# Raw z through DRAM with its silu at the gating, and q, k and v stored by pairs of heads

## The chip, the cores and the metric

The kernel runs on one core of a Trainium2 chip. The metric is device time in microseconds (us), the median of several runs: 641.59 us before the change (three runs, 641.56 to 641.76). Lower is better. Two such medians can be told apart when they differ by about 0.2%, some 1.3 us.

## What is computed

One layer of a diffusion transformer, in fp32, for 1024 latent tokens (a grid of 16 rows by 64 columns), 256 context tokens and a model width of 1024. Cut to what matters:

```python
h  = rmsnorm(x, norm_g) * (1 + scale) + shift          # 1024 tokens
hc = rmsnorm(ctx, norm_g) * (1 + scale_c) + shift_c    # 256 context tokens
q, k, v, za, u, bg, cg, zc = split(h @ w_in)           # eight parts of 512 columns
kc, vc = split(hc @ w_in[:, 512:1536])
q, k, kc = rmsnorm per head                            # 8 heads of 64
# each token sees a window of 8 x 16 neighbours (rotary q and k, learned bias)
# and all 256 context keys (plain q), in one softmax
attn = neighbourhood_attention(q, k, v, kc, vc, rpb) * silu(za)
conv = bg * conv3(cg * u) * silu(zc)
out  = x + gate * (concat([attn, conv]) @ w_out)
```

The change concerns the gate silu(za) of the attention half, and the way by which q, k and v get from the projection to the attention.

## The kernel before, in words

**Precision.** Every fp32 operand of a product is split into a high and a low part (`halves`, line 188: a copy on ScalarE to the rounded high part, a subtraction on VectorE for the low one). A product is three matmuls (`mm3`, line 72). Within a head's scores the two parts lie on the two halves of the 128 partitions: head dimension 64, times two.

**Stages.** First the modulation and the norms. Then the projection (loop at line 1170): for each of four pairs of heads, eight tiles of 128 tokens give 384 columns of q, k and v (`proj_tile`, line 283). Then the attention (line 1287) and at last the output projection (from line 1356 on). Through the projection q, k, v are normed, rotated, transposed, split, and written to DRAM with `spill`, which only notes a transfer; `flush` (line 1166) issues them on SyncE's queue (SP) one tile later. In the attention they come back head by head with `load_k`, `load_q` and `load_v` (lines 944 to 967). q and k of one head fill 64 rows in DRAM; they are loaded twice, to the upper and the lower 64 partitions. v carries a 65th column (ones in the high part, zeros in the low part) that gives the sums of the softmax; it is set once on chip (line 1263), so the transfers of v leave it out and move pieces of 64 floats.

**The quarters.** The attention is a software pipeline over 36 steps, called quarters, four to a head (`quarter`, line 1066). Quarter n computes the scores of group n (`pss` for the window, `pc` for the context), the maxima and exponentials of group n-2, and the products with v of group n-3 (`po`). The order of all instructions on TensorE, ScalarE, VectorE and GpSimd is as written by hand here (`strict`, line 1289); the order of SP's transfers is the scheduler's. Within a quarter ScalarE copies the row maxima (`mg`), which VectorE then subtracts from the scores, and computes the exponentials (`phc`, `sc`, `phl`, `sb`).

**Fillers.** Between these steps TensorE works through the other columns of w_in, in units of 128 columns (`unit`, line 338); one unit has eight ticks, a tick is six matmuls into the bank `pu`. `TICKS` (line 33) says how many ticks each quarter takes: 3 as a rule, 2 in quarters 0, 5 and 8, 4 in quarters 17, 18, 27, 28 and 32, 33. The first four units are the z columns of the four pairs (`attn_group`, line 484), the others belong to three convolution groups (`conv_group`, line 384). Work on the other engines that follows a unit is queued as chores and done at fixed places of a quarter: `do_acts` at its end, `do_dves` near its start.

**The gate.** `attn_group` takes the silu of z from the two banks of a finished unit and stores it (`zs_d`). Once both heads of a pair are done, `gated` (line 1267) advances by one step in each quarter: it loads the sums, takes the reciprocal, stores it, loads silu(z), the attention's output and the reciprocals, multiplies, and stores the product in `y_d`. The last pair is gated in the output stage instead (`put_y`, line 1334).

## Time and profile before

| quantity | value |
|---|---|
| median of three runs | 641.59 us |
| profiled execution, its own time | 643.59 us |
| span in the profile of that execution | 641.8 us |
| TensorE, VectorE, ScalarE, GpSimd busy | 98%, 67%, 50%, 20% of the span |
| DMA, queue of SP | 112,348 packets, 113.23 MB |
| packets under 512 B, all queues | 32,817 of 118,864 |
| attention | from about 270 us to about 535 us of the span |

Times within the span are in us from its start. The profiled execution takes 1.8 us more than its span, and 2.0 us more than the median. In the lists of instructions a row gives start, duration, engine, line, operation, written tile <- read tiles, shape and count; in square brackets stands how long the engine had been idle and on whom it waited. Most lines read L55, that of a helper, so tiles are what to go by. In a table of windows each row gives the stretch, its length, then the busy time of each engine with its count of instructions, the granted clock of TensorE, the busy share of the 16 DMA engines and the bytes moved per second. The matmuls are pipelined, so TensorE looks busy through short gaps; the length of a quarter tells more than its busy time.

### The profile page before, as it was taken

What the parts mean: (1) busy time and instruction counts of PE and PEld (TensorE: products, weight loads), DVE (VectorE), ACT (ScalarE), POOL (GpSimd) and SP (SyncE); (2) the same over time, 40 slices, a digit from 0 to 9 for tenths busy, and PEclk for the clock granted to TensorE, in tenths of its full rate; (3) what the DMA queues carried; (4) which work ended last, traced back from release to release, by engine and by line L of the source; (5) the groups of instructions that cost most, each with busy time, mean ns of one, the idle gap of its engine ahead of it and who ended that gap; (6) DMA issues with size and microseconds to landing.
All of it is one profiled execution on the core that took longest, in us unless ns stands there. A gap on an engine that the chain in (4) does not pass through costs nothing.

```text
span 641.8 us, 10295 instructions
## 1 busy us (share of the span) xinstructions
PE 629.1 (98%) x3480; PEld 537.3 (84%) x3480; DVE 432.3 (67%) x819; ACT 322.5 (50%) x692; POOL 131.5 (20%) x138
## 2 busy tenths in 40 slices
PE   8999999999999999999999999999999999999997
PEld 3477899999899999777688878888888888888885
DVE  1677859665756756458697889988998864565111
ACT  3676835424525444346676648565675644352000
POOL 1205024123123222001111211121111111004421
PEclk9999999999999999999999999999999999999999
DMA  8973647867785897899767758885862223965621
GB/s 319 379 257 97 180 121 259 256 188 206 241 260 165 271 269 218 216 221 223 184 160 195 186 140 212 202 214 149 225 150 88 71 81 128 293 235 198 215 100 49
DMA packets 118864, 125.46 MB, mean 195 GB/s; under 512 B 32817, under 2 KB 89353, under 8 KB 117532
## 3 DMA queue, kind: packets, MB, share of 16 engines
q1 hardware_dynamic: 112348, 113.23, 61.4%
q10 hardware_dynamic: 6208, 11.05, 5.5%
q0 software_dynamic: 256, 0.54, 0.3%
q8 instruction: 27, 0.44, 0.3%
q14 instruction: 25, 0.20, 0.1%
HBM read 88.01 MB, written 38.53 MB: 197 GB/s over the span
## 4 chain that ended last, share of the span: by engine, by line
PE 75%; DMA 10%; DVE 8%; SPq 3%; ACT 2%; issue 1%; ACTq 0%; DVEq 0%
PE pacc L55 21%; PE pu L55 18%; PE acc L55 5%; PE pout L76 5%; PE pout L74 5%; PE pout L75 5%; PE po L55 4%; PE tr L55 4%; PE cacc L55 4%; DMA v<-v_d 4%; DMA k_s<-k_d 3%; DVE mx L55 2%; DVE sb L55 2%; PE pss L55 2%; PE pmx L55 2%; DMA slab<-in_w_ada 2%
## 5 line engine op out<-in xcount | busy, mean ns | idle before, releaser
L55 PE MATMUL pu<-h,uh 128*128 128x512 f32 x544 | 169.0, 392 | 0.0
L55 PE MATMUL pacc<-wh,h 128*128 128x384 f32 x512 | 135.1, 338 | 0.0
L55 PEld LDWEIGHTS pu<-h,uh 128*128 128x128 f32 x544 | 98.2, 188 | 17.0
L55 PE MATMUL pu<-h,ul 128*128 128x512 f32 x272 | 106.3, 391 | 0.0
L55 PEld LDWEIGHTS pacc<-wh,h 128*128 128x128 f32 x512 | 92.8, 188 | 0.1
L55 POOL TENSOR_TENSOR plc<-sc,phc 128x512 fp32r<-128x512 f32 x32 | 42.5, 1327 | 222.8 <-ACT sc L55 111.4
L55 PE MATMUL pacc<-wl,h 128*128 128x384 f32 x256 | 85.6, 335 | 0.0
L55 POOL TENSOR_TENSOR ss<-ss,few 128x4 f32<-128x4 f32 (+1 forms) x40 | 42.0, 1051 | 125.8 <-DVE ss L55 125.4
L55 PEld LDWEIGHTS pu<-h,ul 128*128 128x128 f32 x272 | 51.1, 188 | 11.3
L55 DVE TENSOR_TENSOR mx<-mx,sb 128x384 f32<-128x384 f32 (+1 forms) x64 | 55.5, 876 | 1.9
L75 PE MATMUL pout<-wol,yh 128*128 128x512 f32 x128 | 49.8, 389 | 0.0
L76 PE MATMUL pout<-woh,yl 128*128 128x512 f32 x128 | 49.6, 389 | 0.0
L74 PE MATMUL pout<-woh,yh 128*128 128x512 f32 x128 | 48.3, 389 | 0.0
L55 PEld LDWEIGHTS pacc<-wl,h 128*128 128x128 f32 x256 | 48.1, 188 | 0.1
L55 DVE TENSOR_REDUCE ss<-sq 128x4 f32<-128x260 f32 (+1 forms) x40 | 15.7, 393 | 41.9 <-ACT sq L55 41.9
L55 ACT COPY mg<-pmx 128x256 f32<-128x256 f32 x32 | 12.0, 374 | 61.7 <-PE pmx L55 44.5
L55 ACT ACTIVATE sq<-pacc 128x256 f32<-128x256 f32 x32 | 12.3, 385 | 57.1 <-PE pacc L55 56.6
L1375 DVE TENSOR_TENSOR ot<-pout,gate 128x512 f32<-128x512 f32 x16 | 10.8, 688 | 37.6 <-PE pout L76 35.5
L55 DVE TENSOR_TENSOR pll<-sb,phl 128x768 fp32r<-128x768 f32 (+2 forms) x33 | 29.3, 889 | 7.9 <-ACT sb L55 7.9
L55 DVE TENSOR_TENSOR sc<-sc,mg 128x512 f32<-128x512 f32 x32 | 21.8, 683 | 19.0 <-ACT mg L55 19.0
L1376 POOL TENSOR_TENSOR ot<-ot,xr 128x512 f32<-128x512 f32 x15 | 20.0, 1347 | 67.6 <-DVE ot L1375 66.5
L55 ACT ACTIVATE qn<-pacc,ss 128x64 f32<-128x64 f32 x128 | 30.1, 329 | 4.7 <-issue 2.5
(151 smaller groups left out, 1277.0 us busy)
## 6 DMA issues: line engine op xcount, KB each, us to landing
uraw<-in_w_in SPq DMA_DIRECT2D x34, 256.0 KB
q_d<-qs SPq DMA_DIRECT2D x64, 128.0 KB
k_s<-k_d SPq DMA_DIRECT2D x16, 512.0 KB
q_s<-q_d SPq DMA_DIRECT2D x32, 256.0 KB
wr<-in_w_in SPq DMA_DIRECT2D x40, 192.0 KB
slab<-in_w_ada SPq DMA_DIRECT2D x6, 1024.0 KB
t_d<-btw SPq DMA_DIRECT2D x8, 576.0 KB
bt<-t_d SPq DMA_DIRECT2D x8, 576.0 KB
```

Source lines behind the costliest of these rows:

```text
L55: i = emit(*a, **kw)
L74: i = pe.matmul(ps, ah, bh, start=first, stop=False)
L75: pe.matmul(ps, ah, bl, start=False, stop=False)
L76: pe.matmul(ps, al, bh, start=False, stop=last)
L1375: dve.tensor_tensor(ot, ps, gate[:, cols], ALU.mult)
L1376: (dve if (nh, t) == (1, NB - 1) else pool).tensor_tensor(ot, ot, xr, ALU.add)
```

## The change

- z is copied raw from its bank, each half as soon as it is done, and stored (`z_d`). `gated` loads both halves in its first step; ScalarE takes their silu in place, through a list `held`, either with the next convolution group's silus (pair 0) or by a chore of its own (pairs 1 and 2). Pair 3 takes it in the output stage.
- `gated` makes both multiplications of a half in one step. The gated pairs form a queue; before, a new one took the place of the old one.
- q, k, v and the context's kc and vc are stored by pairs of heads, 128 rows to a transfer. k, q and kc are loaded with one transfer for both partition halves: the rows of high and low parts, or two copies of each row (`twice`), alternate over the partitions.
- v is stored with its 65th column, together with vc; a head's v comes in two transfers with runs of 650 floats in each partition.
- An Exp on a constant column is run on ScalarE three tiles before the end of the projection.
- In quarter 0 one tick of the filler goes ahead of the context's scores; its number of ticks stays 2.

```diff
-    q_d = many("q_d", NH, [2, HD, 4, 2, 256])
-    k_d = many("k_d", NH, [HD, 4, 2, 256])
-    v_d = many("v_d", NH, [P, 4, 2, 2 * HD])
-    kc_d = many("kc_d", NH, [HD, 2, L])
-    vc_d = many("vc_d", NH, [P, 2, 2 * HD])
+    q_d = many("q_d", NPAIR, [P, 2, 4, 2, 256])
+    k_d = many("k_d", NPAIR, [P, 4, 2, 256])
+    v_d = many("v_d", NPAIR, [P, 2, 2, NB + 2, HD + 1])
+    kc_d = many("kc_d", NPAIR, [P, 2, L])
...
+    def spill_v(p, b, vs):
+        spill(v_d[p][:, :, :, b:b + 2].rearrange("p s l b d -> p (s l) (b d)"), vs.rearrange("p s l i d -> p (s l) (i d)"))
...
-            for s in range(2):
-                h, rows = 2 * p + s, slice(64 * s, 64 * s + 64)
-                for l in range(2):
-                    spill(q_d[h][l, :, t0 // 2], qs[rows, l])
-                spill(k_d[h][:, t0 // 2], ks[rows])
+            for l in range(2):
+                spill(q_d[p][:, l, t0 // 2], qs[:, l])
+            spill(k_d[p][:, t0 // 2], ks)
...
     def silus(z):
         out = []
         for half, ps in z:
             out.append(cvp.tile([P, 512], F32, name="zs", tag="ub", bufs=2))
             act.activation(out[half], ps, AF.Silu)
+        while held:
+            for v in held.pop():
+                act.activation(v, v, AF.Silu)
         return out
...
     def attn_group(f):
-        z = []
+        def keep(half, ps):
+            z = cvp.tile([P, 512], F32, name="z", tag="ub", bufs=2)
+            act.copy(z, ps)
+            sp.dma_start(z_d[f][:, half * 512:(half + 1) * 512], z)
+
         for got in unit(z_col(f)):
             if got:
-                z.append(got)
+                chore(lambda got=got: keep(*got))
             else:
                 yield
-        def on_act():
-            for half, zs in enumerate(silus(z)):
-                sp.dma_start(zs_d[f][:, half * 512:(half + 1) * 512], zs)
-        chore(on_act)
...
+    def twice(rows):
+        n = 1
+        for step, size in list(rows.ap)[1:]:
+            n *= size
+        return bass.AP(rows.tensor, rows.offset, [[n, HD], [0, 2], [1, n]])
...
-            for i in range(2):
-                sp.dma_start(self.k[64 * i:64 * i + 64].bitcast(F32), k_d[h])
+            sp.dma_start(self.k[:].bitcast(F32).rearrange("p t l c -> p (t l c)"), twice(k_d[self.p][64 * self.s:64 * self.s + 64]))
...
-            for i in range(2):
-                rows = slice(64 * i, 64 * i + 64)
-                for k in range(2):
-                    sp.dma_start(self.q[rows, k].bitcast(F32).rearrange("p (t c) -> p t c", c=256), q_d[h][i, :, :, k])
-                sp.dma_start(self.kc[rows].bitcast(F32), kc_d[h])
+            for k in range(2):
+                sp.dma_start(self.q[:, k].bitcast(F32).rearrange("p (t c) -> p t c", c=256),
+                             q_d[self.p][64 * self.s:64 * self.s + 64, :, :, k].rearrange("d l t c -> (d l) t c"))
+            sp.dma_start(self.kc[:].bitcast(F32).rearrange("p l c -> p (l c)"), twice(kc_d[self.p][64 * self.s:64 * self.s + 64]))
...
             for l in range(2):
-                for t in range(4):
-                    sp.dma_start(self.v[:, l, 2 * t:2 * t + 2, 0:HD].bitcast(F32),
-                                 v_d[h][:, t, l].rearrange("p (b d) -> p b d", d=HD))
-                sp.dma_start(self.v[:, l, NB:, 0:HD].bitcast(F32), vc_d[h][:, l].rearrange("p (b d) -> p b d", d=HD))
+                sp.dma_start(self.v[:, l].bitcast(F32), v_d[self.p][:, self.s, l])
...
         if gating and next(gating[0], "end"):
-            gating.clear()
+            gating.pop(0)
...
+        if n == 0:
+            next(fill)
+            ticks -= 1
         if live(n):
             heads[n // 4].ctx_scores(n % 4)
...
-        for _ in range(1):
+        for _ in range(n > 0):
             next(fill, None)
...
-        for _ in range(ticks - 1):
+        for _ in range(ticks - (n > 0)):
             next(fill, None)
...
+        if n == NT - 3:
+            act.activation(few[:, 5:6], ones, AF.Exp)
...
+        cols = [slice(half * 512, (half + 1) * 512) for half in range(2)]
+        zs = [ap.tile([P, 512], F32, name="zs", tag="zs", bufs=2) for _ in cols]
+        for v, c in zip(zs, cols):
+            sp.dma_start(v, z_d[f][:, c])
         yield
         dve.reciprocal(ri, ri)
         sp.dma_start(ri_d[f].rearrange("h (x c) -> (h x) c", c=16), ri)
+        held.append(zs)
+        if f:
+            chore(lambda: silus(()))
         yield
-        for half in range(2):
-            cols = slice(half * 512, (half + 1) * 512)
-            zs, tb, rb = (ap.tile([P, 512], F32, name=n, tag=n, bufs=1) for n in ("zs", "tb", "rb"))
-            sp.dma_start(zs, zs_d[f][:, cols])
-            sp.dma_start(tb, o_d[f][:, cols])
+        while held:
+            yield
+        for v, c in zip(zs, cols):
+            tb, rb = (ap.tile([P, 512], F32, name=n, tag=n, bufs=1) for n in ("tb", "rb"))
+            half = cols.index(c)
+            sp.dma_start(tb, o_d[f][:, c])
             load_sums(f, half, rb, sp)
             yield
-            dve.tensor_tensor(zs, zs, rb, ALU.mult)
+            dve.tensor_tensor(v, v, rb, ALU.mult)
+            dve.tensor_tensor(tb, tb, v, ALU.mult)
+            sp.dma_start(y_d[f][:, c], tb)
             yield
-            dve.tensor_tensor(tb, tb, zs, ALU.mult)
-            sp.dma_start(y_d[f][:, cols], tb)
...
-                    gating[:] = [gated(p)]
+                    gating.append(gated(p))
...
                 load_sums(f, half, rb, pool)
+                act.activation(zs, zs, AF.Silu)
                 dve.tensor_tensor(zs, zs, rb, ALU.mult)
```

The transfers of kc and vc in `turn_kc` change in the same way as those of q, k and v. The tiles that hold v before it is stored are now three fixed ones, whose 65th columns GpSimd sets once at the start of the projection.

More of the change, by code (lines that the diff above doesn't have):

```diff
@@ L100, in body @@
     rs_d = many("rs_d", NPAIR, [2, 2, 512])
-    zs_d = many("zs_d", NPAIR, [P, T])
-    q_d = many("q_d", NH, [2, HD, 4, 2, 256])
-    k_d = many("k_d", NH, [HD, 4, 2, 256])
-    v_d = many("v_d", NH, [P, 4, 2, 2 * HD])
-    kc_d = many("kc_d", NH, [HD, 2, L])
-    vc_d = many("vc_d", NH, [P, 2, 2 * HD])
+    z_d = many("z_d", NPAIR, [P, T])
+    q_d = many("q_d", NPAIR, [P, 2, 4, 2, 256])
+    k_d = many("k_d", NPAIR, [P, 4, 2, 256])
+    v_d = many("v_d", NPAIR, [P, 2, 2, NB + 2, HD + 1])
+    kc_d = many("kc_d", NPAIR, [P, 2, L])
     ri_d = many("ri_d", NPAIR, [2, T])
@@ L190, in halves, with next_vs @@
         dve.tensor_tensor(lo, src, dst.bitcast(F32), ALU.subtract)
+    vss = []
+    def next_vs():
+        vss.append(vss.pop(0))
+        return vss[-1]
+    def spill_v(p, b, vs):
+        spill(v_d[p][:, :, :, b:b + 2].rearrange("p s l b d -> p (s l) (b d)"), vs.rearrange("p s l i d -> p (s l) (i d)"))
     def put_v(vs, i, ps):
-        halves(vs[:, :, 0, i], vs[:, :, 1, i], ps.rearrange("p (s d) -> p s d", s=2))
+        halves(vs[:, :, 0, i, :HD], vs[:, :, 1, i, :HD], ps.rearrange("p (s d) -> p s d", s=2))
     def normed(qn, ps, scale, n):
@@ L258, in normed_ctx @@
     def normed_ctx(pp, acc, scales):
-        two = []
-        vs = pp.tile([P, 2, 2, 2, HD], F32R, name="vs", tag="vs", bufs=4)
+        two, vs = [], next_vs()
         for i in range(2):
@@ L276, in put @@
             halves(ks[:, 0], ks[:, 1], pB[:, :256])
-            for s in range(2):
-                h, rows = 2 * p + s, slice(64 * s, 64 * s + 64)
-                spill(kc_d[h], ks[rows])
-                spill(vc_d[h], vs[:, s].rearrange("p l i d -> p l (i d)"))
+            spill(kc_d[p], ks)
+            spill_v(p, NB, vs)
         return put
@@ L475, in conv_group @@
             yield from part()
+    held = []
     def silus(z):
@@ L1158, in body @@
     sq = pp.tile([P, 4, HD + 1], F32, name="sq")
+    vss += [pp.tile([P, 2, 2, 2, HD + 1], F32R, name=f"vs{i}")[:] for i in range(3)]
+    for v in vss:
+        for l in range(2):
+            pool.memset(v[:, :, l, :, HD:HD + 1].bitcast(F32), 1.0 - l)
     pool.memset(sq[:, :, HD:], EPS)
@@ L1213, in body @@
             if n % 2:
-                vs = pp.tile([P, 2, 2, 2, HD], F32R, name="vs", tag="vs", bufs=4)
+                vs = next_vs()
             put_v(vs, (n - 1) % 2, tiles[n - 1][:, 256:384])
@@ L1217, in body @@
                 q, r = divmod(n - 1, NB)
-                for s in range(2):
-                    spill(v_d[2 * q + s][:, r // 2], vs[:, s].rearrange("p l i d -> p l (i d)"))
+                spill_v(q, r - 1, vs)
         if t == at + 1 and n < NT:
@@ L1260, in body @@
     fill_up(prp, 64)
-    for v in vts:
-        for l in range(2):
-            pool.memset(v[:, l, :, HD:HD + 1].bitcast(F32), 1.0 - l)
     gating = []
@@ L1305, in body @@
                 if p < NPAIR - 1:
-                    gating[:] = [gated(p)]
+                    gating.append(gated(p))
                 else:
                     recip(p, ap)
+        for step in gating:
+            for _ in step:
+                do_acts()
+                do_dves()
         for _ in fill:
@@ L1343, in put_y @@
                 rb = op.tile([P, 512], F32, name="rb", tag="rb", bufs=2)
-                act.dma_start(zs, zs_d[f][:, cols])
+                act.dma_start(zs, z_d[f][:, cols])
                 act.dma_start(tb, o_d[f][:, cols])
                 load_sums(f, half, rb, pool)
+                act.activation(zs, zs, AF.Silu)
                 dve.tensor_tensor(zs, zs, rb, ALU.mult)
```

## The prediction, made before the changed kernel was run

> **What bounds the kernel now.** I read the busy times on the page first, then a table of windows cut at the attention's quarters.

> ```profile
> PE 629.1 (98%) x3480; PEld 537.3 (84%) x3480; DVE 432.3 (67%) x819; ACT 322.5 (50%) x692; POOL 131.5 (20%) x138
> ```

> TensorE has next to no idle time, so nothing can be won except where it waits. I cut the windows at each quarter's first row-maximum transpose. The columns are length, then busy time of PE, PEld, DVE, ACT and POOL, clock, DMA share, GB/s.

> ```profile
> 200.00:240.00 40.00, 40.00 (x258) 39.83 (x257) 27.92 (x78) 18.49 (x72) 11.40 (x13) 1.00 0.89 260
> 294.10:302.66 8.56, 7.71 (x43) 6.15 (x42) 7.38 (x11) 5.39 (x9) 1.78 (x2) 1.00 0.90 248
> 309.06:317.65 8.59, 8.11 (x43) 6.37 (x43) 4.81 (x9) 6.11 (x10) 0.10 (x1) 1.00 0.90 209
> 317.65:326.46 8.81, 7.82 (x43) 6.26 (x44) 7.21 (x10) 5.82 (x11) 2.89 (x2) 1.00 0.19 51
> 332.83:340.60 7.77, 7.76 (x49) 6.66 (x50) 5.04 (x9) 6.92 (x11) 1.29 (x1) 1.00 1.08 272
> 340.60:348.48 7.88, 7.72 (x44) 6.42 (x42) 5.43 (x8) 4.71 (x10) 1.29 (x1) 1.00 0.80 209
> 348.48:355.90 7.42, 7.42 (x44) 6.21 (x43) 7.35 (x12) 5.07 (x9) 1.30 (x1) 1.00 0.46 126
> 355.90:363.21 7.31, 7.31 (x43) 6.20 (x42) 6.05 (x10) 4.21 (x7) 1.30 (x1) 1.00 0.65 148
> 370.75:378.95 8.20, 7.67 (x43) 6.30 (x42) 5.12 (x9) 3.28 (x6) 1.30 (x1) 1.00 0.67 153
> 378.95:386.72 7.77, 7.56 (x43) 6.35 (x44) 7.70 (x12) 4.92 (x9) 1.31 (x1) 1.00 0.38 110
> 386.72:394.33 7.61, 7.46 (x43) 6.08 (x42) 7.54 (x14) 5.59 (x10) 1.29 (x1) 1.00 0.68 176
> 434.52:442.06 7.54, 7.54 (x43) 6.42 (x42) 5.53 (x9) 3.89 (x7) 1.30 (x1) 1.00 0.66 172
> 442.06:449.25 7.19, 7.19 (x43) 6.25 (x42) 6.75 (x12) 4.80 (x8) 1.31 (x1) 1.00 0.42 127
> 456.77:464.30 7.53, 7.53 (x49) 6.61 (x48) 7.01 (x10) 5.25 (x9) 1.30 (x1) 1.00 1.05 269
> 471.83:480.79 8.96, 8.84 (x49) 7.34 (x48) 8.86 (x13) 7.96 (x12) 1.38 (x1) 1.00 0.59 176
> 550.00:575.00 25.00, 25.00 (x112) 20.71 (x111) 14.10 (x22) 10.68 (x18) 0.00 (x0) 1.00 0.80 277
> ```

> Four rows serve as clean quarters, where three ticks and TensorE alone set the length: 7.31 us (355.90) for the first of a head, 7.53 (456.77), 7.54 (434.52) and 7.19 (442.06) for the others. Against those of their own kind, quarter 4 (294.10) is 1.25 us too long, quarter 6 (309.06) 1.05, quarter 7 (317.65) 1.62, quarters 9, 10 and 11 0.24, 0.34 and 0.23: **4.73 us** in all. Quarters 14, 15 and 16 (370.75 on) are 0.66, 0.58 and 0.30 too long: **1.54 us**. The projection (200 to 240) and the output stage (550 on) have TensorE busy throughout: no gain there, and whatever the attention saves goes through to the end.

> Next, why those quarters are long: one row of TensorE's timeline, then ScalarE's.

> ```profile
> 271.76 0.74 PE L55 MATMUL pc<-q_s,kc_s 128*128 128x256 f32 x4 [1.05 <-DVE qs L55]
> ```

> ```profile
> 287.39 1.28 ACT L55 ACT_TABLE_LOAD   x1
> 288.69 1.08 ACT L55 ACTIVATE zs<-pu 128x512 f32<-128x512 f32 x2
> 289.66 0.38 ACT L55 COPY mg<-pmx 128x256 f32<-128x256 f32 x1
> 290.55 1.28 ACT L55 ACT_TABLE_LOAD   x1
> 309.16 1.28 ACT L55 ACT_TABLE_LOAD   x1
> 310.46 1.09 ACT L55 ACTIVATE zs<-pu 128x512 f32<-128x512 f32 x2
> 313.31 0.53 ACTq L1043 DMA_DIRECT2D o_d<-ob  x1
> 313.94 0.37 ACT L55 COPY mg<-pmx 128x256 f32<-128x256 f32 x1 [2.40 <-DMA v<-v_d]
> 314.82 1.28 ACT L55 ACT_TABLE_LOAD   x1
> 373.66 0.21 ACTq L1042 DMA_DIRECT2D rs_d<-ob  x1
> 374.46 0.37 ACT L55 COPY mg<-pmx 128x256 f32<-128x256 f32 x1 [4.27 <-DMA rs_d<-ob]
> ```

> Two things delay `mg`, on which the softmax hangs. A silu among the exponentials costs a table load before and one after: 1.28 + 1.09 + 1.28 = 3.65 us of ScalarE. And ScalarE stands still where it has to issue a transfer: 2.40 us at 313.94, 4.27 us at 374.46. The chain of waits shows for whom:

> ```profile
> 301.89 11.40 DMA v<-v_d
> 351.22 1.38 PE pu L55 x6
> 362.14 11.45 DMA v<-v_d
> ```

> 301.89 + 11.40 = 313.29, and the held transfer of `o_d` goes out at 313.31; 362.14 + 11.45 = 373.59, and that of `rs_d` at 373.66. So an issue waits for the landing of some earlier, unrelated transfer, here twice one of v, 11.4 us old. The row between gives a tick: 1.38 us.

> **The change part by part**

> *Quarter 0's tick.* The context's scores wait 1.05 us for VectorE to split the last q. One of quarter 0's two ticks, 1.38 us, now goes before them; their number is the same, so the wait is covered: −1.05 us. Bounds: 0, if the next step is then late by as much, and −1.05.

> *Silu off the early quarters.* Pairs 1 to 3 had their silu at 287, 309 and about 333 us; what is left there is a copy of each half, of the same length. Six table loads leave quarters 2 to 10 (the first Exp's goes to the projection, under TensorE's 40.00 us of 40; if Square needed the other table, it would come back: at most 1.28). Quarter 4's excess follows the batch at 287.39, those of 6 and 7 the batch at 309.16 with the stop at 313, those of 9 and 10 the third.

> *Transfers.* Before, a head loads two transfers of k, four of q, two of kc and ten of v, 18; after, 1 + 2 + 1 + 2 = 6. The stores of the projection fall by half.

> ```profile
> v<-v_d SPq DMA_DIRECT2D x64, 64.0 KB
> k_s<-k_d SPq DMA_DIRECT2D x16, 512.0 KB
> ```

> The 64 v transfers of 64 KB go in runs of 256 bytes; after, each partition gets one run of 2,600 bytes per part. Sixteen of 333 KB take the place of 80, and k's are 1 MB. No row shows such a transfer alone. Its landing lies between 0 and the 11.40 us that v takes in a backlog; I take it nearer the low end, since the bytes are the same while DMA runs above 1.05 in some quarters. With a third of the transfers in the queue, the one that an issue must wait for is older and has mostly landed. So I let both stops of ScalarE go. The stores of v take more, shorter runs (520 bytes for 1,024) where DMA is already at 0.89 (200 to 240); TensorE is covered there by weights loaded tiles ahead, so I price them at 0. If that cover went, I would put two late chunks at about 0.66 each, what the 4.27 us stop cost quarter 14: 1.3 us.

> Of the 4.73 us I take back 4.2, since VectorE at 7.35 of 7.42 in quarter 11 is late next; of the 1.54 us I take 1.2, since VectorE is full in quarters 15 and 16 (7.70 of 7.77, 7.54 of 7.61), although two multiplications of pair 0 leave for later quarters. Bounds: for the first, 1.25 + 0.24 + 0.34 = 1.83 (those with table loads alone) to 4.73; for the second, 0 to 1.54.

> *What comes back.* Pairs 1 and 2 now take their silus by chores after quarters 23 and 30, three-tick quarters, each with two table loads: 3.65 us of ScalarE, with `mg` and the exponentials queued behind, and VectorE behind those. The nearest rows: the convolution's batch at quarter 27 (471.83), which has four ticks: 8.96 − 7.19 − 1.38 = 0.39 us; and quarter 4 with 1.25. I take 0.6 each, nearer the later row since no backlog of transfers is left: +1.2 us, bounds 0.8 and 2.5. Below nothing isn't possible: pure additions to ScalarE. Pair 0's two silus ride with the first convolution's batch at quarter 17, 1.09 us more in a four-tick quarter: +0.1, bounds 0 and 0.4.

> [...] The trace has 290.55 + 1.28 = 291.83 and the next exponential at 291.84, so a switch costs 1.28 us. [...]

> *Pair 3 in the output stage* gets two silus of 0.55 us ahead of its product.

> ```profile
> 574.02 1.29 DVE L1353 TENSOR_TENSOR yl<-tb,yh 128x512 fp32r<-128x512 f32 x2 [0.57 <-ACT yh L1352]
> 575.74 0.39 PE L76 MATMUL pout<-woh,yl 128*128 128x512 f32 x1
> ```

> The first of the two `yl`, half of 1.29 us, is done at about 574.7, and TensorE first uses it at 575.74: 1.0 us of slack for one silu of 0.55 that is not hidden. +0.1 us; bounds 0 and 1.1. z's loads ahead of the gating are issued a quarter before their use, and VectorE's two multiplications in one step sit in quarters with over a microsecond free: 0.

> *Sum:* −1.05 − 4.2 − 1.2 + 1.2 + 0.1 + 0.1 = **−5.05 us**. The profiled span of 641.8 becomes 636.75, that execution's own 643.59 becomes 638.5; from the median of 641.59 it gives **636.5 us**. With the bounds of the two big gains and the late batches, the forecast's own range is 634.3 to 639.4.

> **The rivals**

> *Everything goes.* The whole excess, 4.73 + 1.54 + 1.05 = 7.3 us, also the 0.39 of quarter 27, and the late batches cost nothing, as later quarters have ScalarE busy for 3.9 to 5 of 7.5 us. For it: quarter 23 (442.06) with 4.80 of 7.19. Against: VectorE fills most quarters. 641.6 − 7.7 + 0.2 = 634.1, and to 633 if the two-tick quarters 5 and 8 shrink too.

> *The transfers' stops stay.* An issue still waits for some large transfer, now one of 1 MB. For it: the rule of waiting is unchanged. Then quarters 6, 7 and 14 to 16 keep about 2.6 of their 4.2 us: 641.6 − 5.05 + 2.6 = 639.1.

> *Faster and slower cancel:* ScalarE's stops at quarters 6 and 7 had little to do with it, so that 1.05 + 1.83 = 2.9 us come back, and both late batches cost 1.25: 641.6 − 2.9 + 2.5 + 0.2 = 641.4.

> *Slower: the late batch meets VectorE full.* At quarters 23 and 24 or 30 and 31 ScalarE's 3.65 us push `mg` past the point where VectorE has slack; VectorE is busy 7.01 of 7.53 us in that region (456.77). Then each batch costs as much as that at quarters 6 and 7, 1.05 + 1.62 = 2.67 us; twice 5.3. Costs are then 5.3 + 0.2 = 5.5, and it is slower from the point where the early quarters and 14 to 16 give back under 5.5 − 1.05 = 4.4 of their 6.27 us; with only the 1.05 and the third batch's 0.58 won, 641.6 + 5.3 − 1.6 + 0.2 = 645.5. Against it: quarter 27, where the same batch cost 0.39.

> **How the numbers follow.** Forecast 0.56; everything goes 0.18; stops stay 0.13; cancel 0.06; slower 0.07. The range of 8 in 10 runs from 633.2, near the low end of the second case, to 639.8, past the third. A measurement of this kernel can tell about 0.2%, 1.3 us, from no change: faster 0.87, same 0.06, slower 0.07.

> **What would show it.** In the changed profile: no table load between about 260 and 390 us; quarters 4, 6, 7 and 14 within 0.3 us of the clean lengths; no idle time of ScalarE before `mg` that ends with a transfer; v landing well under 11 us; the wait of 1.05 us before `pc` gone; about 0.6 us more in the quarters after 23 and 30; TensorE without a gap at pair 3 in the output stage. Wrong it would be if the early quarters kept their lengths without table loads (then VectorE bounds them), if ScalarE still stopped for transfers, or if the quarters with the late silus grew by over 1.3 us.

## Result and the profile after

The median of six runs is **637.53 us** (636.79 to 639.57) against 642.03 us before (six runs on the same chip, 641.56 to 642.47): a ratio of 0.9918, with a 95% interval of 0.9892 to 0.9944. The changed kernel is 4.5 us faster. The profiled execution of it took 636.79 us, with a span of 635.0 us; against the 641.8 us of the execution profiled before that is 6.8 us, more than the medians differ. Where the other 2.3 us come from is part of the explanation.

From the page of the changed kernel: busy times, the queue of SP, the chain's shares, and the DMA issues.

```profile
PE 626.1 (99%) x3479; PEld 537.1 (85%) x3480; DVE 436.5 (69%) x819; ACT 324.1 (51%) x699; POOL 130.4 (21%) x140
q1 hardware_dynamic: 96348, 113.38, 53.9%
PE 91%; DVE 6%; ACT 1%; issue 1%; POOL 0%; DVEq 0%; ACTq 0%; POOLq 0%
k_s<-k_d SPq DMA_DIRECT2D x8, 1024.0 KB
q_s<-q_d SPq DMA_DIRECT2D x16, 512.0 KB
v<-v_d SPq DMA_DIRECT2D x16, 325.0 KB
```

The chain of the changed kernel has no DMA share left (10% before). SP's queue moves the same bytes (113.38 MB for 113.23) in 96,348 packets for 112,348.

The table of windows of the changed kernel, cut as before at each quarter's first row-maximum transpose; quarters 4, 6, 7, 10, 14, 15, 25 and 32:

```profile
291.85:299.42 7.57, 7.47 (x43) 6.18 (x42) 6.38 (x10) 5.22 (x9) 1.29 (x1) 1.00 0.46 143
305.79:314.15 8.36, 7.99 (x42) 6.49 (x43) 6.83 (x10) 3.86 (x8) 1.55 (x1) 1.00 0.19 59
314.15:321.34 7.19, 7.19 (x44) 6.26 (x43) 5.70 (x8) 4.90 (x9) 1.30 (x1) 1.00 0.35 112
335.44:342.94 7.50, 7.50 (x43) 6.41 (x42) 5.77 (x9) 4.79 (x9) 1.57 (x1) 1.00 0.18 55
364.96:372.49 7.53, 7.53 (x44) 6.42 (x43) 6.35 (x10) 3.27 (x6) 1.57 (x1) 1.00 0.35 89
372.49:379.68 7.19, 7.19 (x44) 6.26 (x43) 6.31 (x9) 4.90 (x9) 1.30 (x1) 1.00 0.37 106
449.13:456.89 7.76, 7.75 (x49) 6.65 (x50) 7.66 (x12) 5.03 (x9) 1.30 (x1) 1.00 0.90 308
504.28:513.03 8.75, 8.34 (x43) 6.54 (x42) 6.13 (x10) 4.91 (x9) 1.39 (x2) 1.00 0.32 105
```

The first number after the stretch is the quarter's length. Quarters 7, 10, 14 and 15 now have their clean lengths, with TensorE busy throughout, and quarter 4 is 0.26 us above its own (7.31); quarter 6 is not clean. The last two rows are quarters that have become longer. The lengths, cut in the same way in the two profiles (us):

| stretch | before | after | gain |
|---|---|---|---|
| up to the projection | 78.35 | 77.86 | 0.49 |
| projection | 191.88 | 191.82 | 0.06 |
| quarters 0 and 1 | 10.13 | 8.84 | 1.29 |
| quarter 3 | 7.28 | 6.85 | 0.43 |
| quarters 4, 6, 7 | 8.56, 8.59, 8.81 | 7.57, 8.36, 7.19 | 0.99 + 0.23 + 1.62 |
| quarters 9, 10, 11 | 7.77, 7.88, 7.42 | 7.74, 7.50, 7.18 | 0.03 + 0.38 + 0.24 |
| quarters 14, 15, 16 | 8.20, 7.77, 7.61 | 7.53, 7.19, 7.29 | 0.67 + 0.58 + 0.32 |
| quarter 17 | 9.11 | 8.89 | 0.22 |
| quarters 25 and 32 | 7.53, 8.16 | 7.76, 8.75 | −0.23 − 0.59 |
| quarters 27 and 28 | 8.96, 8.66 | 8.53, 9.08 | 0.43 − 0.42 |
| output stage | 86.82 | 86.81 | 0.01 |

### The profile page after: what moved, and what is told of

Its sections match the earlier page's. It is cut to its first block, busy times and chain, and to the rows that moved or that the text cites. A ratio compares the mean times of both kernels' runs of the same rounds, so it can differ in the third digit from the quotient of the medians.

```text
span 635.0 us, 10038 instructions
## 1 busy us (share of the span) xinstructions
PE 626.1 (99%) x3479; PEld 537.1 (85%) x3480; DVE 436.5 (69%) x819; ACT 324.1 (51%) x699; POOL 130.4 (21%) x140
## 2 busy tenths in 40 slices
DMA packets 102863, 125.61 MB, mean 198 GB/s; under 512 B 9649, under 2 KB 71305, under 8 KB 101532
## 3 DMA queue, kind: packets, MB, share of 16 engines
q1 hardware_dynamic: 96348, 113.38, 53.9%
## 4 chain that ended last, share of the span: by engine, by line
PE 91%; DVE 6%; ACT 1%; issue 1%; POOL 0%; DVEq 0%; ACTq 0%; POOLq 0%
PE pu L55 25%; PE pacc L55 21%; PE po L55 7%; PE acc L55 7%; PE tr L55 5%; PE pout L75 5%; PE pout L74 5%; PE pout L76 5%; PE cacc L55 4%; PE pss L55 3%; PE pmx L55 2%; DVE mx L55 2%; PE pc L55 2%; DVE sb L55 2%; PE trA L55 1%
## 5 line engine op out<-in xcount | busy, mean ns | idle before, releaser
L55 PE MATMUL pu<-h,uh 128*128 128x512 f32 x544 | 169.0, 392 | 0.0
L55 PE MATMUL pacc<-wh,h 128*128 128x384 f32 x512 | 135.1, 338 | 0.0
L55 PEld LDWEIGHTS pu<-h,uh 128*128 128x128 f32 x544 | 98.1, 188 | 16.9
L55 PE MATMUL pu<-h,ul 128*128 128x512 f32 x272 | 106.3, 391 | 0.0
L55 PEld LDWEIGHTS pacc<-wh,h 128*128 128x128 f32 x512 | 92.8, 188 | 0.1
L55 POOL TENSOR_TENSOR plc<-sc,phc 128x512 fp32r<-128x512 f32 x32 | 43.0, 1345 | 215.5 <-ACT sc L55 159.0
L55 PE MATMUL pacc<-wl,h 128*128 128x384 f32 x256 | 85.6, 334 | 0.0
L55 POOL TENSOR_TENSOR ss<-ss,few 128x4 f32<-128x4 f32 (+1 forms) x40 | 41.4, 1037 | 126.3 <-DVE ss L55 126.1
L55 DVE TENSOR_TENSOR mx<-mx,sb 128x384 f32<-128x384 f32 (+1 forms) x64 | 59.4, 936 | 2.0
L55 PEld LDWEIGHTS pu<-h,ul 128*128 128x128 f32 x272 | 51.1, 188 | 11.3
L76 PE MATMUL pout<-woh,yl 128*128 128x512 f32 x128 | 49.5, 389 | 0.0
L55 PEld LDWEIGHTS pacc<-wl,h 128*128 128x128 f32 x256 | 48.1, 188 | 0.1
L55 DVE TENSOR_REDUCE ss<-sq 128x4 f32<-128x260 f32 (+1 forms) x40 | 15.8, 394 | 42.4 <-ACT sq L55 42.4
L55 ACT ACTIVATE sq<-pacc 128x256 f32<-128x256 f32 x32 | 12.3, 384 | 54.4 <-PE pacc L55 53.9
L55 ACT COPY mg<-pmx 128x256 f32<-128x256 f32 x32 | 11.9, 372 | 51.9 <-PE pmx L55 45.3
L55 ACT COPY sc<-pc 128x512 f32<-128x512 f32 x32 | 18.8, 588 | 25.5 <-PE pc L55 25.5
L55 ACT ACTIVATE qn<-pacc,ss 128x64 f32<-128x64 f32 x128 | 30.0, 329 | 3.0 <-issue 2.5
L55 DVE TENSOR_TENSOR pll<-sb,phl 128x768 fp32r<-128x768 f32 (+2 forms) x33 | 28.4, 861 | 4.5 <-ACT sb L55 4.5
## 6 DMA issues: line engine op xcount, KB each, us to landing
q_s<-q_d SPq DMA_DIRECT2D x16, 512.0 KB
```

What stands on the lines that cost most here:

```text
L55: i = emit(*a, **kw)
L76: pe.matmul(ps, al, bh, start=False, stop=last)
```

## The experiments

The theories at the start were two. Mine: three separate covers were taken off TensorE's waits, each worth its own time, so that the parts add up. The rival: one part carries the gain. Every comparison below has its own runs of the kernel before, on the same chip (medians 642.0, 642.4 and 642.1); lengths of quarters come from the profiled execution of each kernel. The code cuts show the lines that matter; the rest of each edit is left out.

**The tick alone**, in the kernel before:

```diff
+        if n == 0:
+            next(fill)
+            ticks -= 1
```

> The kernel before with the filler's tick moved ahead of the context's scores in quarter 0, and nothing else. My theory (the wait of 1.05 us is covered and nothing takes its place): 1.0 us faster than before, no wait before pc, quarters 2 to 35 as before. Rival (the next step is late instead): within 0.3 us of before, with as much idle time later in quarters 0 to 2.

642.13 us (640.03 to 646.60), ratio 0.9997 [0.9974, 1.0020]. Quarters 0 and 1 fall from 10.13 to 8.82 us, as in the full change, but the total doesn't show it: the interval reaches down to −1.7 us, so 1.3 us may be there or may be lost behind it (quarters 10 and 11 were 0.17 and 0.32 us longer here). Quarters 14 and 15 were clean in this execution, 7.53 and 7.19 us, though nothing near them was changed; the next two kernels have them clean too, one of them with all transfers as before. What the profile of before shows there was thus an accident of that one execution. Stops as such were not: this execution has one of 2.54 us in quarter 6, where before had 2.40, and one of 3.22 us in quarter 10 (342.91, behind `rs_d`), where before had none.

**The late silu alone**, in the kernel before: `attn_group`, `silus`, `gated`, `put_y` and the early Exp as changed, all transfers of q, k and v as they were.

```diff
-        chore(on_act)
+                chore(lambda got=got: keep(*got))
...
+        held.append(zs)
+        if f:
+            chore(lambda: silus(()))
```

> The kernel before with only the silu moved: raw z stored, silu at the gating, Exp run once in the projection; transfers of q, k, v and the tick as before. Theory of two causes (table loads and stops of ScalarE by transfers add up): quarters 3 and 4 lose 1.4 us, 10 and 11 about 0.5, 7 only a part of its 1.62 us, 14 to 16 stay long at about 1.5 us; the quarters after 23 and 30 gain 0.2 to 0.6 each. In all 2 to 3 us faster. Rival (table loads alone): all of quarters 3 to 17 reach the clean lengths, 5 us faster. Rival (transfers alone): no change of quarters 4 to 16, and slower by 0.8 us.

645.02 us (643.35 to 651.00), ratio 1.0043 [1.0018, 1.0067]: **slower**. The profile is of the slowest of these twelve executions (651.00), 6.0 us above their median, so it shows the stops larger, or more of them, than most executions had. Quarters 3, 4, 10 and 11 are as short as in the full change, so the table loads are worth what they should be. But ScalarE stands still twice; its timeline in this kernel:

```profile
312.49 0.50 ACTq L1046 DMA_DIRECT2D rs_d<-ob  x1
313.64 0.37 ACT L55 COPY mg<-pmx 128x256 f32<-128x256 f32 x1 [5.99 <-DMA rs_d<-ob]
439.78 0.20 ACTq L1046 DMA_DIRECT2D rs_d<-ob  x1
440.63 0.37 ACT L55 COPY mg<-pmx 128x256 f32<-128x256 f32 x1 [8.07 <-DMA rs_d<-ob]
```

The chain of waits of the same kernel says what each issue waited for (start, length, what):

```profile
300.71 11.70 DMA k_s<-k_d
425.11 14.60 DMA zs<-z_d
```

300.71 + 11.70 = 312.41, and `rs_d` goes out at 312.49; 425.11 + 14.60 = 439.71, and it goes out at 439.78. Quarters 6 and 7 become 11.01 and 9.26 us, 22 and 23 become 11.94 and 9.19. A smaller wait of the same kind, for `rb<-ri_d` (464.03 + 8.73 = 472.76), goes with quarter 26 at 8.59 us instead of 7.53.

The first stop was there before too, half covered. In the kernel before ScalarE stood still for 2.40 us at that place, behind 2.38 us of one table load and two silus (309.16 to 311.54; the other load came after `mg`): 4.78 us together. Here quarters 3 and 4 are 1.41 us shorter, and the stop is 5.99 us. `mg` ran 43.71 us after the attention's first `pss` before (270.23 to 313.94), and runs 43.92 us after it here (269.72 to 313.64). A landing sets its time, of v before and of k here, with or without a silu, and what the quarters ahead had saved is spent in waiting for it. The second stop is new: both halves of z are now loaded in one step, and one of them takes 14.60 us to land in the backlog.

**The transfers alone**, in the kernel before: the silu stays early, no tick is moved.

```diff
-            for i in range(2):
-                sp.dma_start(self.k[64 * i:64 * i + 64].bitcast(F32), k_d[h])
+            sp.dma_start(self.k[:].bitcast(F32).rearrange("p t l c -> p (t l c)"), twice(k_d[self.p][64 * self.s:64 * self.s + 64]))
```

> The kernel before with only the transfers of q, k, v, kc and vc changed; silu and tick as before. Theory of two causes: quarters 14 to 17 reach the clean lengths (1.8 us), ScalarE has no stop for a transfer at quarters 6 and 13, quarter 7 loses about half of its 1.62 us, quarter 4 stays long by about 1 us because its table loads stay. In all 2 to 3.5 us faster. Rival (transfers alone): 5 us faster, quarter 4 clean. Rival (table loads alone): within 0.5 us of before.

642.29 us (641.75 to 644.04), ratio 0.9993 [0.9976, 1.0011]: nothing. Quarter 7 is clean at 7.19 us and no stop of ScalarE is left, but quarters 17 and 18 are 10.22 and 9.67 us, where before had 9.11 and 8.86. VectorE's and SP's timelines in this kernel:

```profile
397.12 0.69 DVE L55 TENSOR_TENSOR zs<-zs,rb 128x512 f32<-128x512 f32 x1 [2.50 <-DMA zs<-zs_d]
```

```profile
385.84 1.24 SPq L963 DMA_DIRECT2D q_s<-q_d  x2
387.13 0.62 SPq L956 DMA_DIRECT2D k_s<-k_d  x1
388.43 0.47 SPq L1282 DMA_DIRECT2D zs<-zs_d  x1
```

The gate's half of 256 KB, issued one quarter before its use, now stands behind q (2 x 512 KB) and k (1 MB), and lands 8.6 us after its issue. So quarters 6, 7 and 11 win 0.23, 1.62 and 0.21 us against before, and quarters 17 and 18 lose 1.11 and 0.81. That the full change loads both halves of z earlier is what it needs here; the next kernel shows it.

**All but the late silu**: the full change, with silu at the old place and the result of it stored and loaded ahead as z is.

```diff
-        held.append(zs)
-        if f:
-            chore(lambda: silus(()))
```

> The changed kernel with the silu put back to its old place: taken from the finished unit, stored, and loaded ahead by the gating in its first step as the change does; no Exp in the projection. Transfers, tick and the gating's new steps stay. If the late silu is itself a gain: quarters 3 and 4 are 1.4 us longer than in the changed kernel, 10 and 11 about 0.6, quarter 7 clean (its excess was the stop for a transfer), the quarters after 23 and 30 shorter by 0.8 in all; 1 to 1.5 us slower than the changed kernel, 3 to 4 faster than before. Rival (the gain lies in transfers and loading ahead alone): the time of the changed kernel, within 0.5 us. Rival (the silu carries most): within 1 us of before.

639.75 us (638.99 to 641.21), ratio 0.9955 [0.9940, 0.9971]. Quarters 17 and 18 are 8.91 and 8.94: with the load ahead, the wait of the last kernel is gone. Against the full change, quarters 3, 4, 10, 16 and 24 are longer by 0.43, 0.97, 0.37, 0.30 and 0.64 us and quarter 25 shorter by 0.20. The place of the silu is worth 2.4 us (ratios 0.9955 and 0.9918) once the transfers are as changed; two kernels of this chip with the late silu, shown below, are at 637.20 and 637.13, 2.6 us less than this one. Not all of it is table loads: the 0.64 us of quarter 24 follow quarter 23, where VectorE here takes both multiplications of a half in one step, and the late silu moves these to other quarters.

So the parts do not add up. Tick +0.1, silu +3.0, transfers +0.3 against the kernel before; together −4.5. My first theory fell, and so did the rival: each of the two big parts has a cost that goes away in the full change, where the other is done too.

**Why ScalarE's stops go.** My reason in the prediction was the number of transfers. If so, v in ten pieces must bring them back:

```diff
-                sp.dma_start(self.v[:, l].bitcast(F32), v_d[self.p][:, self.s, l])
+                for t in range(5):
+                    b = slice(2 * t, 2 * t + 2)
+                    sp.dma_start(self.v[:, l, b].bitcast(F32), v_d[self.p][:, self.s, l, b])
```

> The changed kernel with each head's v loaded in ten transfers of two blocks, in runs of 520 bytes, instead of two; everything else stays. Theory (the number of transfers in the queue makes ScalarE's issue of rs_d and o_d wait for the landing of an older one): stops of over 3 us before mg come back at one to three quarters, each making its quarter 1 to 4 us longer; 1 to 5 us slower than the changed kernel. Rival (the short runs of 256 bytes were the cause): no stop, the changed kernel's time within 0.7 us.

637.20 us (636.91 to 637.67), ratio 0.9914 [0.9899, 0.9929], and no stop. The theory of the number fell. Next came the length of the runs: pieces of 64 floats again, the 65th column set once on chip, in ten transfers a head and in two.

```diff
-                sp.dma_start(self.v[:, l].bitcast(F32), v_d[self.p][:, self.s, l])
+                for t in range(5):
+                    b = slice(2 * t, 2 * t + 2)
+                    sp.dma_start(self.v[:, l, b, 0:HD].bitcast(F32), v_d[self.p][:, self.s, l, b, 0:HD])
```

> The changed kernel with each head's v loaded as before: ten transfers in runs of 64 floats (256 bytes), without the 65th column, which is set once on chip. q, k, kc and all else as changed. The theory of the number of transfers fell: ten transfers in runs of 520 bytes cost nothing. New theory (the 256-byte runs keep the DMA engines busy, and ScalarE's issue waits for their landing): packets under 512 bytes rise by about 20,000, stops of several us before mg return, 2 to 6 us slower than the changed kernel. Rival (the transfers of q and k, merged, were what helped): within 0.7 us of the changed kernel.

```diff
-                sp.dma_start(self.v[:, l].bitcast(F32), v_d[self.p][:, self.s, l])
+                sp.dma_start(self.v[:, l, :, 0:HD].bitcast(F32), v_d[self.p][:, self.s, l, :, 0:HD])
```

> As the kernel with v in ten transfers of 256-byte runs, but with two transfers to a head. If the runs alone are the cause: stops of ScalarE return, 2 to 6 us slower than the changed kernel. If number and runs are needed together: no stop of over 3 us, within 1 us of the changed kernel.

637.36 us (637.11 to 637.68), ratio 0.9927 [0.9914, 0.9941], and 637.15 us (636.82 to 638.52), ratio 0.9929 [0.9914, 0.9945]: no stop in either. Then the other half undone, q, k and kc by head and in halves, v as changed:

```diff
-            sp.dma_start(self.k[:].bitcast(F32).rearrange("p t l c -> p (t l c)"), twice(k_d[self.p][64 * self.s:64 * self.s + 64]))
+            for i in range(2):
+                sp.dma_start(self.k[64 * i:64 * i + 64].bitcast(F32), k_d[h])
```

> The changed kernel with q, k and kc stored by head and loaded twice in halves, as before; only v in its new form. Theory (v's runs are the cause): no stop of over 3 us before mg, within 1 us of the changed kernel. Rival (q, k and kc matter as much): at least half of the 4.5 us lost again, with stops at some quarters.

638.14 us (637.66 to 638.63), ratio 0.9941 [0.9925, 0.9956], no stop. Beside them ran the changed kernel once more:

> The changed kernel itself, for comparison on the same chip as the three others: 4 to 6 us faster than before; its quarters as in its first profile within 0.1 us, but for those that wait on transfers.

637.89 us (637.39 to 639.15), ratio 0.9939 [0.9923, 0.9955]. All four agree with it within their intervals. Either half is enough. What they share is seen in the DMA share over quarters 0 to 4, 270 to 300 us (second number from the end); the rows of before, of the late silu alone, of the kernel with v alone changed, and of the full change:

```profile
270.00:300.00 30.00, 27.49 (x149) 22.68 (x148) 19.76 (x34) 17.65 (x29) 3.00 (x3) 1.00 0.91 225
```

```profile
270.00:300.00 30.00, 28.35 (x152) 23.85 (x151) 22.33 (x36) 15.20 (x28) 3.93 (x3) 1.00 0.90 226
```

```profile
270.00:300.00 30.00, 29.39 (x162) 24.84 (x160) 22.75 (x36) 16.30 (x30) 3.95 (x3) 1.00 0.83 242
```

```profile
270.00:300.00 30.00, 29.39 (x161) 24.84 (x160) 22.97 (x37) 15.97 (x29) 3.93 (x3) 1.00 0.62 197
```

The kernels at 0.90 and 0.91 have the stops, and so has the tick alone at 0.93; all the others, with 0.49 (transfers alone) to 0.83, have none. (Three waits of 1.9 to 2.4 us before `mg` in the changed kernel are put down to `o_d`, but end with TensorE's transposes, at 336.77 and 366.29 for `mg` at 336.80 and 366.33: ordinary waits.) So the stops seem to belong to a backlog that is worked off late, not to one kind of transfer. The two go together in these runs, but no run changed the backlog alone, and why an issue waits for an unrelated landing stays open; nor was the late silu tried with the tick and the old transfers.

**Why quarter 6 stays long.** VectorE's timeline in the changed kernel over quarter 5, then TensorE's in quarter 6:

```profile
299.84 0.43 DVE L55 TENSOR_REDUCE rm<-pmx 128x2 f32<-128x256 f32 x1 [0.64 <-PE pmx L55]
300.18 1.28 DVE L55 TENSOR_TENSOR ul<-uraw,uh 128x512 fp32r<-128x512 f32 x2
...
304.17 2.06 DVE L55 TENSOR_TENSOR mx<-mx,sb 128x384 f32<-128x384 f32 x2
306.15 0.95 DVE L55 TENSOR_TENSOR pll<-sb,phl 128x768 fp32r<-128x768 f32 x1
307.02 0.42 DVE L55 TENSOR_REDUCE rm<-pmx 128x2 f32<-128x256 f32 x1
```

```profile
306.29 0.33 PE L55 MATMUL pmx<-ci,mx 128*128 128x128 f32 x1 [0.20 <-DVE mx L55]
307.49 0.43 PE L55 MATMUL pmx<-ci,rm 128*128 128x128 f32 x2 [0.17 <-DVE rm L55]
```

After 299.84 VectorE has no idle time until quarter 6 is under way, and TensorE waits for its `mx` and then its `rm`. Quarter 5 has two ticks and leaves VectorE too little time. A third tick tests it; it was taken from quarter 17 so that the sum stays.

```diff
-TICKS = [2, 3, 3, 3, 3, 2, 3, 3, 2] + 2 * (8 * [3] + 2 * [4]) + 3 * [3] + [4, 4, 3, 2]
+TICKS = [2, 3, 3, 3, 3, 3, 3, 3, 2] + 9 * [3] + [4] + 8 * [3] + 2 * [4] + 3 * [3] + [4, 4, 3, 2]
```

> The changed kernel with three ticks in quarter 5 instead of two and three in quarter 17 instead of four. After the change quarter 6 is still 8.36 us long, though no table load and no stop of ScalarE is near it. Theory (VectorE's work of quarter 5, with two weight splits, does not fit in its 6.4 us, and the rest makes quarter 6 wait): quarter 5 takes 7.5 to 7.7 us, quarter 6 falls to about 7.6, quarter 17 takes 7.6; 0.5 to 0.8 us faster than the changed kernel. Rival (quarter 6 has a wait of its own, or VectorE's lag only moves on): quarter 6 stays above 8.1 or quarter 7 grows, and the time is that of the changed kernel within 0.3 us.

640.07 us (638.81 to 641.29), ratio 0.9952 [0.9934, 0.9970]. The windows of this kernel, quarters 5, 6 and 16:

```profile
300.92:308.45 7.53, 7.53 (x49) 6.62 (x48) 7.05 (x10) 4.67 (x8) 1.29 (x1) 1.00 0.84 300
308.45:315.98 7.53, 7.53 (x44) 6.41 (x43) 5.77 (x9) 3.79 (x7) 1.59 (x1) 1.00 0.17 55
381.54:391.78 10.24, 7.95 (x44) 6.05 (x42) 8.03 (x14) 8.02 (x13) 1.30 (x1) 1.00 0.78 254
```

Quarter 6 is clean at 7.53, so VectorE's lag was its cause; the batch of silus was not, since with that batch still there quarter 6 takes 8.36 (transfers alone) and 8.33 us (all but the late silu). But units now end a tick earlier, and in quarter 16 TensorE waits 2.12 us for a bank that the silus still read. With the tick taken from quarter 12 instead:

```diff
+TICKS = [2, 3, 3, 3, 3, 3, 3, 3, 2] + 3 * [3] + [2] + 4 * [3] + 2 * [4] + 8 * [3] + 2 * [4] + 3 * [3] + [4, 4, 3, 2]
```

> The changed kernel with three ticks in quarter 5 and two in quarter 12, so that units and quarters stand as before from quarter 13 on. With the tick taken from quarter 17 the next unit's first matmul had to wait 2.12 us in quarter 16 for a bank that the silus still read, since the unit ended a tick earlier in its quarter. Theory: no such wait now; quarter 5 takes 7.53, quarter 6 7.53, quarter 12 6.0 to 6.5; 0.4 to 0.8 us less than the changed kernel. Rival (VectorE lags wherever there are two ticks): quarter 13 grows by as much as quarter 6 lost, and nothing is won.

637.13 us (636.74 to 638.60), ratio 0.9917 [0.9901, 0.9934]. Quarters 5, 6, 12 and 13 are 7.54, 7.52, 6.36 and 7.74, together 0.4 us less than in the changed kernel: quarter 6 lost 0.84 us, and quarter 13, now behind a quarter of two ticks, grew by 0.20. The total can't be told from that of the changed kernel.

**Pair 1 without table loads of its own**: its silus wait for the second convolution group's batch, at quarter 27.

```diff
-        if f:
+        if f == 2:
```

> The changed kernel with pair 1's silus left to the second convolution group's batch instead of a chore of their own: two table loads less, after quarter 23. Theory (a late batch costs 0.2 to 0.6 us): quarters 23 to 25 reach the clean lengths, 0.3 us less; quarters 27 and 28 grow by at most 0.4 for two silus more; time that of the changed kernel within 0.5 us. Rival (the late batches cost a microsecond or more each): 1 us faster or more.

640.01 us (637.42 to 640.78), ratio 0.9950 [0.9932, 0.9969]. Quarters 24, 25, 28 and 32 are 7.30, 7.55, 8.66 and 7.94 for 7.47, 7.76, 9.08 and 8.75: 1.6 us less. But pair 2, in the queue behind pair 1, is gated too late, and the windows of the attention's last stretch and of the output stage show it:

```profile
512.36:544.67 32.31, 30.76 (x152) 25.00 (x151) 16.68 (x28) 16.11 (x25) 4.70 (x7) 1.00 0.44 133
544.67:633.61 88.94, 87.25 (x384) 71.94 (x384) 32.59 (x50) 18.56 (x31) 20.04 (x15) 1.00 0.56 186
```

They were 30.30 and 86.81 us in the changed kernel: 4.1 us more, so the move loses.

## Why the prediction was right, and where not

**The sum.** −5.05 us was forecast, the medians differ by 4.5, and 637.53 lies in the likeliest case's own range. Sign and size were right; several of the steps behind them were not, and that their errors cancel is luck: the 1.2 us of quarters 14 to 16 were for the most part never to be had, and quarter 0, quarter 17 and the late batches together came out about 0.9 us better than priced. The range of 634.3 to 639.4 doesn't follow from the bounds either: with all of them at one end the sum gives 635.3 or 641.4.

**Quarter 0's tick.** −1.05 forecast; 1.29 us less in quarters 0 and 1. Right in the profile; alone it did not show in the total.

**Silu off the early quarters.** 4.2 of 4.73 us were forecast; the six quarters on that list gave 3.49, and quarter 3, which was not on it, 0.43. But not all of this is the silu's: with the silu at its old place and the transfers changed, quarters 6, 7 and 11 are as short (8.33, 7.22 and 7.18), so 2.09 of the 3.49 us came with the transfers; with the silu went quarters 3, 4, 10 and 16. A step that failed is the 1.05 us of quarter 6, which I put down to the batch at 309.16: the batch went, and 0.83 of it stayed, because VectorE is late from quarter 5. Quarter 9's 0.24 us stayed too, at 7.73 to 7.77 in all runs; it also follows a quarter of two ticks, so 7.53 was not its clean length. I had named "VectorE bounds them" as what could go wrong, but did not look at it where a two-tick quarter comes before. The early Exp did its work: the changed kernel's ScalarE has a table load at 242.13 and none until 386.64.

**Transfers.** The forecast was that both stops go, and they went. The reason, fewer transfers so that the awaited one is older, was not what decides: with v in ten transfers they stay away too. And the weight was missing: without this part the silu's move costs 3 us (and no tick was moved there). I had that case as "the stops stay" at 639.1. The late silu alone gave 645.02 (with neither tick nor merged transfers), because I had counted the table loads and the stop behind them as two gains, while one covers the other, and because z's own load became an awaited transfer, landing after 14.60 us where v's took 11.45 in the profile of before. The 1.2 us taken in quarters 14 to 16 was an accident for the most part: the tick alone had quarters 14 and 15 clean. The two profiled executions stand 1.56 us above and 0.74 below their medians, which makes the 2.3 us between 6.8 and 4.5. Those 1.25 us and the 0.49 ahead of the projection place 1.74 of them; where the rest lies is not shown. The stores of v in 520-byte runs cost 0, as forecast.

**What comes back.** +1.2 us for two late batches. Quarter 25 grew by 0.23 us and quarter 32 by 0.59, 0.8 in all, the low bound; but read against the kernel with the silu at its old place, that is not the price of the batches. There quarter 32 takes 8.76 us as well. VectorE's rows in that kernel in quarter 31, then TensorE's at quarter 32:

```profile
501.89 0.68 DVE L55 TENSOR_TENSOR zs<-zs,rb 128x512 f32<-128x512 f32 x1
502.61 0.69 DVE L55 TENSOR_TENSOR tb<-tb,zs 128x512 f32<-128x512 f32 x1
506.00 1.67 DVE L55 TENSOR_TENSOR mx<-mx,sb 128x384 f32<-128x384 f32 x2
507.73 0.33 PE L55 MATMUL pmx<-ci,mx 128*128 128x128 f32 x1 [0.20 <-DVE mx L55]
```

The two multiplications of a half, now in one step, stand ahead of the `mx` for which TensorE waits. The prediction put that step at 0; it goes with 0.60 us in quarter 32 there, and with the 0.59 us more that quarter 24 takes there than before. Against that kernel the late silu adds 0.20 us in quarter 25, 0.44 in quarter 28 (9.08 for 8.64, after a quarter 27 with a batch and both multiplications) and nothing in quarter 32; against before, quarters 27 and 28 cancel. So a term of 1.2 was about 0.8 in size, with a part of its cause left out. Pair 0's silus at quarter 17 were priced at 0.1 and the output stage at 0.1; neither shows (quarter 17 is shorter by 0.22). ScalarE's timeline of the changed kernel at quarter 17's batch:

```profile
242.13 1.28 ACT L55 ACT_TABLE_LOAD   x1
386.64 1.28 ACT L55 ACT_TABLE_LOAD   x1
387.93 1.09 ACT L55 ACTIVATE zs<-pu 128x512 f32<-128x512 f32 x2
388.90 1.15 ACT L55 ACTIVATE zs<-zs 128x512 f32<-128x512 f32 x2
```

386.64 + 1.28 = 387.92, and the silu starts at 387.93: 0.01 us behind the load.

**The rivals.** "Slower" asked for 2.67 us a batch; the quarters behind the batches grew by 0.23 and 0.59. "Everything goes" failed at quarter 6 and at the late batches. "Cancel" had ScalarE's stop matter little in quarter 7; it gave back all 1.62.

## What to carry to other kernels

Before adding up the parts of a change, ask of each which wait it leans on: here moving the silu was worth 2.4 us with the transfers changed and cost 3.0 with the old ones, where ScalarE stood still for 5.99 and 8.07 us with a store to issue. Merging transfers pushed back a load of 256 KB queued behind them, which landed 8.6 us after its issue, and that load had to be issued earlier along with it. And an excess seen in one profiled execution needs a second execution, or a nearby kernel with the same code there, before it goes into a sum.

## What the runs showed of the hardware beyond expectation

```profile
318.09:327.35 9.26, 9.06 (x43) 7.77 (x44) 6.21 (x10) 5.22 (x10) 1.48 (x1) 0.82 0.15 43
```

and in finer cuts:

```profile
317.00:320.00 3.00, 1.71 (x11) 1.40 (x11) 2.44 (x4) 0.31 (x1) 0.53 (x1) 0.91 0.00 0
320.00:323.00 3.00, 3.00 (x13) 2.86 (x12) 2.27 (x3) 0.93 (x3) 0.00 (x0) 0.52 0.00 0
323.00:327.00 4.00, 4.00 (x22) 3.33 (x21) 2.56 (x5) 3.94 (x8) 1.48 (x1) 1.00 0.35 98
```

The stop was paid twice in this execution: quarter 7 takes 9.26 us with TensorE busy for 9.06 of them, at a mean clock of 0.82 (a clean one takes 7.19). At the second stop of this kernel TensorE idles 4.24 us before 445.08, and the clock is 0.50 from 446 to 449. In quarter 16 of the kernel with a third tick in quarter 5, where TensorE waits 2.12 us, it is 1.00 over the whole quarter. No run varied a stop alone, so what makes the clock fall isn't shown.

**VectorE's `mx` is longer beside GpSimd's product.** The pair of `mx` takes 1.15 us at 275.70 in the changed kernel, with GpSimd idle (its row at 282.94 has 23.23 us of idle time ahead of it), and 2.06 us at 304.17, where GpSimd's product runs from 303.93 to 305.22. VectorE's row, then GpSimd's two:

```profile
275.70 1.15 DVE L55 TENSOR_TENSOR mx<-mx,sb 128x384 f32<-128x384 f32 x2
```

```profile
282.94 1.33 POOL L55 TENSOR_TENSOR plc<-sc,phc 128x512 fp32r<-128x512 f32 x1 [23.23 <-ACT sc L55]
...
303.93 1.29 POOL L55 TENSOR_TENSOR plc<-sc,phc 128x512 fp32r<-128x512 f32 x1 [6.22 <-ACT sc L55]
```

Of the 24 such pairs in the changed kernel's attention only the first has no overlap with GpSimd's product; the other 23 take 1.67 to 2.20 us, and the extra time is 0.5 to 1.05. No run took the product away, so it isn't shown that the product is the cause; if it is, it has a part in quarter 6 being late.

**Short runs did not show in the time.** v in ten pieces of 256 bytes has 31,153 packets under 512 bytes, where the changed kernel has 9,649, and its time can't be told from it (637.36 and 637.89), though DMA's busy share from 270 to 300 us is 0.77 for 0.62.
